# Two rows normalised inside the output projection, an earlier place for the first sigmoid, and four subtractions moved from GpSimd to VectorE

## The chip, the core and the metric

The kernel runs on one core of a Trainium2 chip. The core has a matmul engine (TensorE, PE in the profile, with its weight loads as PEld), a vector engine (VectorE, DVE), an engine for activation functions (ScalarE, ACT), a general engine (GpSimd, POOL) and a queue that only starts transfers (SyncE, SP). Each engine works through its own queue in order, and engines wait for each other by semaphores. A tile lies in SBUF, or, where PE writes it, in one of eight PSUM banks. The metric is the device time of one execution in microseconds; less is better.

## The reference

Two layers work on 512 tokens of 1024 features. Layer 0 projects the normalised tokens, runs a recurrence over them and a short convolution, and brings 2048 features back to 1024 with an output projection. Layer 1 is a convolution module. Around the border between the two the reference computes

```python
y = concatenate([ya * silu(za), yb * silu(zb)]) @ w_out       # layer 0, output projection
x = x + gate * rms_norm(y, g_post[0])                         # "post"
h = rms_norm(x, g_pre[1]) * (1 + scale) + shift               # "norm"
u, gl, z = split(h @ w_in, 3)                                 # layer 1, input projection
a = dwconv(u * sigmoid(gl), dw_w, 64) + dw_b                  # over segments of 64 tokens
```

Then follow a layer norm of `a`, `silu(a) * silu(z)`, and the second output projection. All is float32.

## The kernel before

**Precision.** A product of two float32 matrices is made of three matmuls (`mm3`, line 59): each operand is split into a high part, which ScalarE makes with a cast (line 126), and a low part, which is the operand less the high part (line 127). Line 127 subtracts on the engine that `env["lo"]` names: VectorE, or, for the weights of part 0 of the first 512 columns of layer 1, GpSimd (line 1115).

**Output projection.** `outproj` (line 130) multiplies two of the four rows of 128 tokens at a time: 16 steps (`ks`) of 12 matmuls of 512 columns, summed in four banks. The first call makes rows 0 and 1, in the banks `mm0`, `mm1` and the two of `at`; the second (line 1056) makes rows 2 and 3 in `uh0`, `uh1` and the two of `zo`, and starts with the three weight blocks that the first still holds. Each step loads 128 rows of the weight `wr` and of the activations `yr` through SP's queue, splits them into `wh`, `wl` and `y`, and has three sets of buffers for it.

**Rows.** Behind the second projection in the text stands a loop over the four rows (line 1060). `post` (line 1018) loads `x`, squares the row's two banks on ScalarE with a running sum, takes the square root (in `rstd`, line 1009) and the reciprocal, multiplies and adds on VectorE, and writes the row `x1d` for the end of layer 1. `norm` (line 1035) does the same with the new row: square, square root, reciprocal, product `xn`; then eight transposes of 128 by 128 on PE into the banks `at` (`h1t`, line 1046), eight activations that scale and shift (`hf`, line 1049), and the split into `h1h` and `h1l`.

**Layer 1.** For each of four groups of 512 columns (`n`), the weights are loaded and split (`wc...`, part 1 for `gl` and part 0 for `u`). Then, for each row `m`, 24 matmuls for part 1 and 24 for part 0 give two banks `pu`; the sigmoid of the first times the second is `a` (lines 1132 and 1133), which is split into `ah` (lines 1138 and 1139). The convolution is done with a short transform: `forward` multiplies `ah` with `dfc` into `px`, VectorE multiplies this with the transformed kernel `What` into `pr`, and `back` transforms it into `pc`. Both are put into a list, `late`, and run one after each of the next row's two parts. Banks for `pu` go round `mm0`, `mm1`, `uh0`, `uh1` (`dense`); `px` has the banks `zo` and `pc` the banks `at`.

**What sets the order.** The framework places instructions in the engines' queues ahead of time: whatever is earlier in the text comes first where it can run, and later work fills what the plan of times leaves empty. So the order in a queue isn't the order of the text, but the text gives the priority. Two means overrule it: `pinned()` (line 559) chains matmuls in the written order, used for `forward`, `back` and the products from `n + m = 2` on; and `tc.issue_after(ins)` places what is written in its block behind `ins` on the engine of `ins`. Tiles with one tag share a number of buffers (`BUFS`, line 992); a new tile waits until the old one's last reader is done.

Of the kernel before, what the change touches and what calls it, by code (L numbers as in the profile page):

```python
# [17 lines left out]
KT = 8  # L18
# [33 lines left out]
def kernel(ctx: ExitStack, tc: tile.TileContext, I: dict, out: bass.AP):  # L52
# [6 lines left out]
    def mm3(o, ah, al, bh, bl, start, stop, go=mm):  # L59
        go(o, ah, bh, start, False)  # L60
        go(o, ah, bl, False, False)
        go(o, al, bh, False, stop)
# [64 lines left out]
        env["lo"].tensor_tensor(out=lo, in0=raw, in1=hi, op=ALU.subtract)  # L127
        return hi, lo

    def outproj(m0, tags, ks, held, early=lambda k: (None, None, None)):  # L130
        acc = [[bank(f"o{m0 + m}{n}", tags[2 * m + n]) for n in range(2)] for m in range(2)]
        for k in ks:
            y, yr, ws = early(k)
            if y is None:
                y = op.tile([P, 512], F32R, tag="y", name=f"y{m0}_{k}", bufs=4)
            yh, yl = y[:, 0:256], y[:, 256:512]
            if (m0, k) == (0, 7):
                hilo(oT7[:, 0:256], None, yh, yl, None)
            else:
                if yr is None:  # L140
                    yr = op.tile([P, 256], F32, tag="yr", name=f"yr{m0}_{k}", bufs=4)
                hilo(ysp[k, :, m0 * P : m0 * P + 2 * P], yr, yh, yl)
            if k not in held:
                if ws is None:
                    ws = [op.tile([P, D], F32, tag="wr", name=f"wr{m0}_{k}", bufs=3)] + [
                        op.tile([P, D], F32R, tag="w", name=f"w{x}{m0}_{k}", bufs=6) for x in "hl"]
                held[k] = hilo(wo[k * P : (k + 1) * P, :], *ws)
            wh, wl = held[k]
            for m in range(2):
                ms = slice(m * P, (m + 1) * P)  # L150
                for n in range(2):
                    ns = slice(n * 512, n * 512 + 512)
                    mm3(acc[m][n], yh[:, ms], yl[:, ms], wh[:, ns], wl[:, ns], k == ks[0], k == ks[-1])
        return acc

    l0, rs = ExitStack(), ExitStack()
# [833 lines left out]
    with ExitStack() as l1:  # L990
# [3 lines left out]
        def lt(tag, name, dt=F32):  # L994
            return (lq if tag in ("xr", "pr") else lp).tile([P, 512 if tag in ("a", "pr") else D], dt, tag=tag, name=name,
                                                            bufs=BUFS[tag])
# [5 lines left out]
        def big(name, shape, dt=F32):  # L1002
            return lp.tile(shape, dt, tag=name, name=name)

        def dense(name):
            flip["mm"] = (flip["mm"] + 1) % 4
            return bank(name, ("mm0", "mm1", "uh0", "uh1")[flip["mm"]])

        def rstd(ssq, eps):
            S.activation(ssq[:, 2:3], ssq[:, 2:3], AF.Sqrt, bias=epsr[:, eps : eps + 1], scale=1.0 / D)  # L1010
            V.reciprocal(ssq[:, 3:4], ssq[:, 2:3])

        def gate_rows(layer):
            g = lq.tile([P, D], F32, tag="gg", name="gg1") if layer else lt("wz", "gg0")
# [3 lines left out]
        def post(m, pss, gg):  # L1018
            xr = lt("wz", f"x{m}")
            nc.gpsimd.dma_start(xr, I["x"][0, m * P : (m + 1) * P, :])  # L1020
            ssq = lp.tile([P, 4], F32, tag="ssq", name=f"ssqa{m}", bufs=4)
            t = lp.tile([P, D], F32, tag="pt", name=f"pta{m}", bufs=2)
            for n in range(2):
                S.activation(t[:, n * 512 : n * 512 + 512], pss[n], AF.Square, accum_out=ssq[:, n : n + 1])
            V.tensor_tensor(out=ssq[:, 2:3], in0=ssq[:, 0:1], in1=ssq[:, 1:2], op=ALU.add)
            rstd(ssq, 0)
            for n in range(2):
                sl = slice(n * 512, n * 512 + 512)
                V.scalar_tensor_tensor(out=t[:, sl], in0=pss[n], scalar=ssq[:, 3:4], in1=gg[:, sl],
                                       op0=ALU.mult, op1=ALU.mult)  # L1030
            V.tensor_tensor(out=xr, in0=xr, in1=t, op=ALU.add)
            nc.sync.dma_start(x1d[m], xr)
            return xr

        def norm(m, x1):
            ssq = lp.tile([P, 4], F32, tag="ssq", name=f"ssqb{m}", bufs=4)
            xn = lp.tile([P, D], F32, tag="pt", name=f"xn{m}", bufs=2)
            S.activation(xn, x1, AF.Square, accum_out=ssq[:, 2:3])
            rstd(ssq, 0)
            V.tensor_scalar(out=xn, in0=x1, scalar1=ssq[:, 3:4], scalar2=None, op0=ALU.mult)  # L1040
            for k4 in range(2):
                pt = bank(f"h1t{m}{k4}", "at")
                hf = lt("a", f"hf{m}{k4}").rearrange("p (k c) -> p k c", c=P)
                for k in range(4):
                    kt = 4 * k4 + k
                    T.transpose(pt[:, k * P : (k + 1) * P], xn[:, kt * P : (kt + 1) * P], ident)
                for k in range(4):
                    kt = 4 * k4 + k
                    S.activation(hf[:, k, :], pt[:, k * P : (k + 1) * P], AF.Identity, bias=modc1[:, kt : kt + 1],  # L1049
                                 scale=gsc1[:, kt : kt + 1])  # L1050
                ms = slice(m * P, (m + 1) * P)
                S.copy(h1h[:, 4 * k4 : 4 * k4 + 4, ms], hf)
                V.tensor_tensor(out=h1l[:, 4 * k4 : 4 * k4 + 4, ms], in0=hf, in1=h1h[:, 4 * k4 : 4 * k4 + 4, ms],
                                op=ALU.subtract)

        acc = outproj(2, ("uh0", "uh1", "zo", "zo"), ORDER[-3:] + ORDER[:-3], {k: held[k] for k in ORDER[-3:]})
        h1h = big("h1h", [P, KT, SEQ], F32R)
        h1l = big("h1l", [P, KT, SEQ], F32R)
        gg = gate_rows(0)
        for m in range(4):  # L1060
            x1 = post(m, (acc0 + acc)[m], gg)
            norm(m, x1)

        rs.close()
        lq = rs.enter_context(tc.tile_pool(name="lq", bufs=1, reuse_waits="tile", side="right"))
        w1_in = I["od_w_in"][0]
        dfw = lt("a", "dfw")[:, :NPROD]
        dfc = lt("pt", "dfc", F32R)
        dfh, dfl = dfc[:, :NPROD], dfc[:, NPROD : 2 * NPROD]
        dbe = big("dbe", [NPROD, 1])  # L1070
        dinv = big("dinv", [NPROD, 64])
        What = lq.tile([NPROD, EC], F32, tag="What", name="What")
        nc.gpsimd.dma_start(What, dwd)
        nc.gpsimd.dma_start(dfw, I["dfw"])
        S.copy(dfh, dfw)
        V.tensor_tensor(out=dfl, in0=dfw, in1=dfh, op=ALU.subtract)
        nc.gpsimd.dma_start(dbe, I["dbe"])
        nc.gpsimd.dma_start(dinv, I["dinv"])
        cres = [[lt("xr", f"cres{m}{q}") for q in range(2)] for m in range(4)]
        stats = big("stats", [P, 4, 4, 6])  # L1080
        tp = pinned()
        late = []

        def dft_stages(n, m, ahl):
            pr = [lt("pr", f"pr{n}{m}{s}") for s in range(2)]
# [20 lines left out]

            return forward, back

        for n in range(4):
            ws = {}  # L1110
            for part, tag in ((1, "wa"), (0, "wb")):
                for kt in range(0, KT, 2):
                    c0 = part * EC + n * 512
                    src = w1_in[kt * P : (kt + 2) * P, c0 : c0 + 512].rearrange("(a p) c -> p a c", p=P)
                    env["lo"] = G if n == 0 and part == 0 else V
                    w = split(src, f"wc{n}{part}{kt}", tag)
                    env["lo"] = V
                    for q in range(2):
                        ws[part, kt + q] = [t[:, q * 512 : q * 512 + 512] for t in w]
            for m in range(4):  # L1120
                ms = slice(m * P, (m + 1) * P)
                pp = []
                for part in (1, 0):
                    pu = dense(f"pu{n}{m}{part}")
                    for kt in range(KT):
                        wh, wl = ws[part, kt]
                        mm3(pu, h1h[:, kt, ms], h1l[:, kt, ms], wh, wl, kt == 0, kt == KT - 1, mm if n + m < 2 else tp)
                    pp.append(pu)
                    if late:
                        late.pop(0)()  # L1130
                a = lt("a", f"a{n}{m}")
                S.activation(a, pp[0], AF.Sigmoid)
                V.tensor_tensor(out=a, in0=pp[1], in1=a, op=ALU.mult)  # L1133
                ah = lt("wz", f"ah{n}{m}", F32R)
                ahl = [ah[:, 512 * s : 512 * s + 512] for s in range(2)]
                for s in range(2):
                    hr, lr = slice(64 * s, 64 * s + 64), slice(64 - 64 * s, 128 - 64 * s)
                    S.copy(ahl[s][hr], a[hr])  # L1138
                    V.tensor_tensor(out=ahl[s][lr], in0=a[hr], in1=ahl[s][hr], op=ALU.subtract)
                late.extend(dft_stages(n, m, ahl))  # L1140
        while late:
            late.pop(0)()
        for m in range(4):
# [159 lines left out]
```

## Time and profile before

| what | value |
|---|---|
| median of three runs | 1467.58 us (1464.46 to 1472.43) |
| the profiled execution | 1466.0 us, its span 1464.2 us |
| busy, share of the span | PE 96%, DVE 67%, ACT 51%, POOL 9% |
| granted clock of PE, mean | 0.978 |
| end of the second output projection | 1041.9 us into the span |

The span is what the profiler saw of the program's instructions; 1.8 us of the profiled execution's time lie outside it. A busy time is the time in which at least one instruction of the engine runs. "Line" numbers are those of the kernel before; a helper's line stands for all that call it, so the tile's name (output first, then the inputs) tells which work it is. The word behind an arrow is what an instruction waited for last.

### The profile page before, as it was taken

The numbers are of one execution on the slowest core, as the hardware profiler recorded it, in microseconds if no ns is written. First come the engines' busy times: TensorE is split into PE (matmuls) and PEld (weight loads), VectorE is DVE, ScalarE is ACT, GpSimd is POOL, SyncE is SP. The second block draws the span as 40 slices with busy tenths as digits, with TensorE's granted clock in tenths as the row PEclk, the third lists the DMA queues.
The fourth block names the chain that finished last, engine by engine and source line by source line (L and its number), as shares of the span: only waits on it lengthen the run. The fifth ranks groups of instructions, "written<-read, shape, count | busy, mean of one in ns | idle before, by whom it ended". The sixth has DMA issues, their size and how long they took to land. (4 is left out here: it accounts for less than half of the span.)

```text
span 1464.2 us, 29746 instructions
## 1 busy us (share of the span) xinstructions
PE 1408.5 (96%) x11921; PEld 1012.7 (69%) x11921; DVE 985.3 (67%) x2290; ACT 750.0 (51%) x1516; POOL 129.1 (9%) x250
## 2 busy tenths in 40 slices
PE   6899999999999999999999999999889999999998
PEld 1464677878776766666666666777767777788876
DVE  2675597567698989999999997557535535544333
ACT  4536364353655666656756655446643423463222
POOL 2023210000110101111011000011100000000000
PEclk9999999979897999999999999999989999999999
DMA  9755433312232312232222222468503303123322
GB/s 322 217 171 161 153 108 101 96 44 76 76 89 75 95 57 73 69 97 60 75 81 79 65 63 76 165 224 297 185 16 115 109 8 115 58 90 98 101 87 86
DMA packets 137626, 158.54 MB, mean 108 GB/s; under 512 B 15375, under 2 KB 104143, under 8 KB 137369
## 3 DMA queue, kind: packets, MB, share of 16 engines
q1 hardware_dynamic: 121104, 106.47, 23.5%
q0 software_dynamic: 15312, 48.99, 10.5%
q8 instruction: 93, 1.52, 0.4%
q10 hardware_dynamic: 1072, 1.19, 0.2%
q14 instruction: 45, 0.37, 0.1%
HBM read 138.33 MB, written 18.28 MB: 107 GB/s over the span
## 5 line engine op out<-in xcount | busy, mean ns | idle before, releaser
L57 PE MATMUL o<-wh,y 128*128 128x512 f32 x248 | 79.1, 396 | 0.0
L57 PE MATMUL pal<-ARl,BKl 64*128 64x128 f32 x512 | 58.1, 307 | 6.9 <-DVE xtmpc L654 2.9
L656 DVE TENSOR_TENSOR Yl<-Yl,xtmpl 128x126 f32<-128x126 f32 (+22 forms) x248 | 62.6, 252 | 2.7
L654 DVE TENSOR_TENSOR xtmpl<-Xl,Yl 128x126 f32<-128x126 f32 (+22 forms) x248 | 62.4, 252 | 2.7
L57 PEld LDWEIGHTS pal<-ARl,BKl 64*128 64x128 f32 x512 | 43.2, 195 | 26.3 <-issue 7.2
L1138 ACT CAST ah<-a 64x512 fp32r<-64x512 f32 x32 | 19.8, 619 | 72.9 <-DVE a L1133 72.4
L57 PE MATMUL zol<-UV,E 64*64 64x64 f32 (+1 forms) x1024 | 54.0, 221 | 0.2 <-ACT UV L762 0.2
L57 PE MATMUL o<-wl,y 128*128 128x512 f32 x124 | 49.6, 400 | 4.3 <-DVE wl L127 4.3
L127 DVE TENSOR_TENSOR wl<-wr,wh 128x1024 fp32r<-128x1024 f32 x28 | 38.1, 1361 | 23.1 <-ACT wh L126 22.7
L57 PEld LDWEIGHTS o<-wh,y 128*128 128x128 f32 x248 | 45.9, 188 | 9.6
L762 ACT COPY UV<-uh 64x128 f32<-64x128 f32 x128 | 33.4, 261 | 33.4 <-PE uh L57 25.8
L57 PE MATMUL zol<-Hl,ARl 64*64 64x64 f32 x896 | 50.2, 230 | 0.3
L57 PEld LDWEIGHTS zol<-Hl,ARl 64*64 64x64 f32 x896 | 35.0, 133 | 20.3 <-issue 16.7
L57 PEld LDWEIGHTS uh<-UV,BKt 128*64 128x64 f32 x704 | 26.7, 138 | 28.6 <-ACT UV L762 22.9
L599 DVE TENSOR_TENSOR E<-pal,maskE 128x512 f32<-128x512 f32 x64 | 43.1, 686 | 4.5 <-PE pal L57 4.2
L1133 DVE TENSOR_TENSOR a<-pu,a 128x512 f32<-128x512 f32 x16 | 11.0, 690 | 51.3 <-PE pu L57 49.0
L1094 DVE SCALAR_TENSOR_TENSOR pr<-px,dbe,What 119x512 f32<-119x512 f32 x32 | 22.6, 747 | 32.6 <-PE px L57 32.4
L57 PEld LDWEIGHTS zol<-UV,E 64*64 64x64 f32 (+1 forms) x1024 | 42.3, 136 | 2.6 <-ACT UV L762 2.0
L126 ACT CAST wh<-wr 128x1024 fp32r<-128x1024 f32 x28 | 29.4, 1051 | 23.5 <-DMA wr<-in_ev_w_out_dram 14.3
L873 POOL DMA_DIRECT2D mwr<-in_mod_w_dram x56 | 29.9, 539 | 113.9 <-PE uh L57 67.1
L769 DVE SCALAR_TENSOR_TENSOR Hl<-uh,PCl,HPl 128x64 f32<-128x64 f32 x112 | 26.5, 278 | 19.9 <-PE uh L57 9.7
L57 PE MATMUL uh<-UV,BKt 128*64 128x64 f32 x704 | 36.7, 234 | 2.2 <-ACT UV L762 2.2
(947 smaller groups left out, 4260.3 us busy)
## 6 DMA issues: line engine op xcount, KB each, us to landing
mwr<-in_mod_w_dram POOLq DMA_DIRECT2D x56, 256.0 KB, 3.8
wr<-in_ev_w_out_dram SPq DMA_DIRECT2D x28, 512.0 KB, 4.9
ectx<-in_mod_w_dram SPq DMA_DIRECT2D x12, 512.0 KB, 4.7
wrk<-in_ev_w_in_dram SPq DMA_DIRECT2D x16, 256.0 KB, 3.0
wrv<-in_ev_w_in_dram SPq DMA_DIRECT2D x16, 256.0 KB, 4.7
wrr<-in_ev_w_in_dram SPq DMA_DIRECT2D x16, 256.0 KB, 2.8
wrza<-in_ev_w_in_dram SPq DMA_DIRECT2D x16, 256.0 KB, 2.9
wrcg<-in_ev_w_in_dram SPq DMA_DIRECT2D x16, 256.0 KB, 2.9
```

The lines of the kernel that those rows point to most:

```text
L57: return T.matmul(o, lhsT, rhs, start=start, stop=stop)
L126: S.copy(hi, raw)
L127: env["lo"].tensor_tensor(out=lo, in0=raw, in1=hi, op=ALU.subtract)
L599: V.tensor_tensor(out=E[:, h, z * NLAT + c0 : z * NLAT + c0 + m, :], in0=pas[h], in1=maskE[:, z * (1 + h) : z * (1 + h) + 1, 0:x].to_broad ...
L654: V.tensor_tensor(out=tv, in0=X[:, :i, i : i + 1].to_broadcast([P, i, m]), in1=Y[:, i : i + 1, c0:].to_broadcast([P, i, m]), op=ALU.mult)
L656: V.tensor_tensor(out=Y[:, :i, c0:], in0=Y[:, :i, c0:], in1=tv, op=ALU.add)
L762: u_ = S.copy(UV[ZR[1 - h], i : 2 * nch - i : 2 * nch - 1 - 2 * i, ZR[h]], uh[ZR[1 - h], 0:2, :])
L769: h_ = V.scalar_tensor_tensor(out=Hn[:, z, :], in0=uh[:, 2 + z, :], scalar=PC[z][:, i : i + 1], in1=HP[:, z, :], op0=ALU.mult, op1=ALU.add)
L873: nc.gpsimd.dma_start(mws[q], I["mod_w"][layer, kt * P : (kt + 1) * P, c0 : c0 + 512])
L1094: V.scalar_tensor_tensor(out=pr[s][:NPROD], in0=px[s][:NPROD], scalar=dbe[:, 0:1], in1=What[:, n * 512 : n * 512 + 512], op0=ALU.add, op1= ...
L1133: V.tensor_tensor(out=a, in0=pp[1], in1=a, op=ALU.mult)
L1138: S.copy(ahl[s][hr], a[hr])
```

## The change

Five things, and the text they stand in:

1. `outproj` takes a table `between`, from a step to something that is run behind this step's matmuls. The second call has `rows(0)` (post and norm of row 0) behind step 13, its ninth, and `rows(1)` behind step 15, its eleventh. What these need (`h1h`, `h1l`, the gate row) is made ahead of the call; so are the small constants of the transform (`dfw`, `dfc`, `dbe`, `dinv`), which get tiles of their own.
2. The loop over `n` is taken apart into `weights`, `products` and `gated`. The weights and products of the first group and row are written ahead of row 2's and row 3's post and norm.
3. The first `gated` stands between row 3's post and its norm, and behind row 3's first square root (on ScalarE) and row 3's sum (on VectorE), which `post` leaves in `ordered`.
4. The pool that holds `What`, `cres` and `pr` is opened after row 3's norm, and `What` is loaded there.
5. `env["lo"]` stays on VectorE for all weights of layer 1.

```diff
-    def outproj(m0, tags, ks, held, early=lambda k: (None, None, None)):
+    def outproj(m0, tags, ks, held, early=lambda k: (None, None, None), between={}):
...
                     mm3(acc[m][n], yh[:, ms], yl[:, ms], wh[:, ns], wl[:, ns], k == ks[0], k == ks[-1])
+            if k in between:
+                between[k]()
...
         def rstd(ssq, eps):
-            S.activation(ssq[:, 2:3], ssq[:, 2:3], AF.Sqrt, bias=epsr[:, eps : eps + 1], scale=1.0 / D)
+            r_ = S.activation(ssq[:, 2:3], ssq[:, 2:3], AF.Sqrt, bias=epsr[:, eps : eps + 1], scale=1.0 / D)
             V.reciprocal(ssq[:, 3:4], ssq[:, 2:3])
+            return r_
...
-            V.tensor_tensor(out=xr, in0=xr, in1=t, op=ALU.add)
+            ordered[:] = [r_.ins, V.tensor_tensor(out=xr, in0=xr, in1=t, op=ALU.add).ins]
...
-        acc = outproj(2, ("uh0", "uh1", "zo", "zo"), ORDER[-3:] + ORDER[:-3], {k: held[k] for k in ORDER[-3:]})
+        w1_in = I["od_w_in"][0]
         h1h = big("h1h", [P, KT, SEQ], F32R)
         h1l = big("h1l", [P, KT, SEQ], F32R)
         gg = gate_rows(0)
-        for m in range(4):
-            x1 = post(m, (acc0 + acc)[m], gg)
-            norm(m, x1)
-
-        rs.close()
-        lq = rs.enter_context(tc.tile_pool(name="lq", bufs=1, reuse_waits="tile", side="right"))
...
-        dfc = lt("pt", "dfc", F32R)
+        dfc = big("dfc", [P, 2 * NPROD + 2], F32R)
...
+        def rows(m):
+            norm(m, post(m, acc0[m], gg))
+
+        order2 = ORDER[-3:] + ORDER[:-3]
+        acc = outproj(2, ("uh0", "uh1", "zo", "zo"), order2, {k: held[k] for k in ORDER[-3:]},
+                      between={order2[8]: lambda: rows(0), order2[10]: lambda: rows(1)})
...
-                    env["lo"] = G if n == 0 and part == 0 else V
                     w = split(src, f"wc{n}{part}{kt}", tag)
-                    env["lo"] = V
...
+        weights(0)
+        flip["mm"] = 3
+        pp = products(0, 0)
+        norm(2, post(2, acc[0], gg))
+        x1 = post(3, acc[1], gg)
+        with tc.issue_after(ordered[0]), tc.issue_after(ordered[1]):
+            first = gated(0, 0, pp)
+        norm(3, x1)
+        rs.close()
+        lq = rs.enter_context(tc.tile_pool(name="lq", bufs=1, reuse_waits="tile", side="right"))
+        What = lq.tile([NPROD, EC], F32, tag="What", name="What")
+        nc.gpsimd.dma_start(What, dwd)
+        cres = [[lt("xr", f"cres{m}{q}") for q in range(2)] for m in range(4)]
+        stats = big("stats", [P, 4, 4, 6])
+        late.extend(dft_stages(0, 0, first))
+        for n in range(4):
+            if n:
+                weights(n)
+            for m in range(n == 0, 4):
+                late.extend(dft_stages(n, m, gated(n, m, products(n, m))))
```

`products(n, m)` holds the two loops of matmuls and the calls of `late` between them, as they stood; `gated(n, m, pp)` holds the sigmoid, the product and the split into `ah`, as they stood.

More of the change, by code (lines that the diff above doesn't have):

```diff
@@ L1025, in post @@
             V.tensor_tensor(out=ssq[:, 2:3], in0=ssq[:, 0:1], in1=ssq[:, 1:2], op=ALU.add)
-            rstd(ssq, 0)
+            r_ = rstd(ssq, 0)
             for n in range(2):
@@ L1059 @@
         gg = gate_rows(0)
-        for m in range(4):
-            x1 = post(m, (acc0 + acc)[m], gg)
-            norm(m, x1)
-        rs.close()
-        lq = rs.enter_context(tc.tile_pool(name="lq", bufs=1, reuse_waits="tile", side="right"))
-        w1_in = I["od_w_in"][0]
+        ordered = []
         dfw = lt("a", "dfw")[:, :NPROD]
-        dfc = lt("pt", "dfc", F32R)
+        dfc = big("dfc", [P, 2 * NPROD + 2], F32R)
         dfh, dfl = dfc[:, :NPROD], dfc[:, NPROD : 2 * NPROD]
-        dbe = big("dbe", [NPROD, 1])
+        dbe = big("dbe", [P, 8])[:NPROD, 0:1]
         dinv = big("dinv", [NPROD, 64])
-        What = lq.tile([NPROD, EC], F32, tag="What", name="What")
-        nc.gpsimd.dma_start(What, dwd)
         nc.gpsimd.dma_start(dfw, I["dfw"])
@@ L1078 @@
         nc.gpsimd.dma_start(dinv, I["dinv"])
-        cres = [[lt("xr", f"cres{m}{q}") for q in range(2)] for m in range(4)]
-        stats = big("stats", [P, 4, 4, 6])
+        def rows(m):
[3 more added lines that the diff above has]
+                      between={order2[8]: lambda: rows(0), order2[10]: lambda: rows(1)})
         tp = pinned()
         late = []
+        ws = {}
         def dft_stages(n, m, ahl):
@@ L1107, in dft_stages, with weights @@
             return forward, back
-        for n in range(4):
-            ws = {}
+        def weights(n):
             for part, tag in ((1, "wa"), (0, "wb")):
@@ L1114 @@
                     src = w1_in[kt * P : (kt + 2) * P, c0 : c0 + 512].rearrange("(a p) c -> p a c", p=P)
-                    env["lo"] = G if n == 0 and part == 0 else V
                     w = split(src, f"wc{n}{part}{kt}", tag)
-                    env["lo"] = V
                     for q in range(2):
                         ws[part, kt + q] = [t[:, q * 512 : q * 512 + 512] for t in w]
[L1120 to L1140, printed above, removed]
@@ new lines, in products, with gated @@
+        def products(n, m):
+            ms = slice(m * P, (m + 1) * P)
+            pp = []
+            for part in (1, 0):
+                pu = dense(f"pu{n}{m}{part}")
+                for kt in range(KT):
+                    wh, wl = ws[part, kt]
+                    mm3(pu, h1h[:, kt, ms], h1l[:, kt, ms], wh, wl, kt == 0, kt == KT - 1, mm if n + m < 2 else tp)
+                pp.append(pu)
+                if late:
+                    late.pop(0)()
+            return pp
+        def gated(n, m, pp):
+            a = lt("a", f"a{n}{m}")
+            S.activation(a, pp[0], AF.Sigmoid)
+            V.tensor_tensor(out=a, in0=pp[1], in1=a, op=ALU.mult)
+            ah = lt("wz", f"ah{n}{m}", F32R)
+            ahl = [ah[:, 512 * s : 512 * s + 512] for s in range(2)]
+            for s in range(2):
+                hr, lr = slice(64 * s, 64 * s + 64), slice(64 - 64 * s, 128 - 64 * s)
+                S.copy(ahl[s][hr], a[hr])
+                V.tensor_tensor(out=ahl[s][lr], in0=a[hr], in1=ahl[s][hr], op=ALU.subtract)
+            return ahl
```

## The prediction

> **What bounds the kernel now.** I read the page first, then the windows around the edited code, then the waits of the matmul engine there, then the chain of waits and the timelines of each engine. The page says that TensorE is the bound:
>
> ```profile
> span 1464.2 us, 29746 instructions
> PE 1408.5 (96%) x11921; PEld 1012.7 (69%) x11921; DVE 985.3 (67%) x2290; ACT 750.0 (51%) x1516; POOL 129.1 (9%) x250
> ```
>
> So an edit of the schedule can only win back time in which PE stands still, or runs slowly. The windows (us, then busy time of PE, PEld, DVE, ACT, POOL, the granted clock, the DMA share, GB/s) find both in the edited stretch: the second output projection ends at about 1042, and layer 1's first products follow.
>
> ```profile
> 1000.00:1020.00 20.00, 18.07 (x78) 14.02 (x77) 18.96 (x24) 15.36 (x28) 6.31 (x3) 1.00 0.88 303
> 1020.00:1040.00 20.00, 17.60 (x76) 13.91 (x77) 14.21 (x15) 9.49 (x14) 4.98 (x2) 1.00 0.76 262
> 1040.00:1060.00 20.00, 18.64 (x91) 14.73 (x90) 8.48 (x17) 13.07 (x37) 1.10 (x2) 1.00 0.51 142
> 1060.00:1080.00 20.00, 14.75 (x60) 9.79 (x58) 10.36 (x16) 12.96 (x29) 0.55 (x1) 0.82 0.08 30
> 1080.00:1100.00 20.00, 20.00 (x82) 14.96 (x82) 7.10 (x9) 5.73 (x8) 0.00 (x0) 0.92 0.00 0
> ```
>
> The shortfalls of the first four rows are 1.93 + 2.40 + 1.36 + 5.25 = 10.9 us, and the granted clock is 0.82 and then 0.92 after the largest. The waits of PE between 980 and 1090 (total us, times, longest) name them:
>
> ```profile
> PE px L57 <- DVE ah L1139: 4.3, 1, 4.3
> PE o L57 <- DVE wl L127: 4.3, 4, 1.7
> PE h1t L1046 <- ACT hf L1049: 1.2, 1, 1.2
> PE pc L57 <- DVE pr L1094: 0.8, 1, 0.8
> PE pu L57 <- ACT h1h L1052: 0.2, 1, 0.2
> ```
>
> These five are all there is to win as idle time. What comes on top is the slow clock behind the first, which the chain of waits shows (start, us, what):
>
> ```profile
> 1074.61 2.25 PE px L57 x4
> ...
> 1077.65 2.62 PE pc L57 x8
> 1080.28 7.12 PE pu L57 x24
> 1087.39 0.89 PE px L57 x3
> 1088.28 5.80 PE pu L57 x24
> 1094.08 1.01 PE pc L57 x8
> ```
>
> The same three pieces cost 0.89, 1.01 and 5.80 us one row of tokens later. So the slow clock costs (2.25 - 0.89) + (2.62 - 1.01) + (7.12 - 5.80) = 4.3 us.
>
> **Part 1: GpSimd subtracts no weights.** Four subtractions for the columns of part 0 move from GpSimd to VectorE. GpSimd's four, and the VectorE instructions that ran beside them, with one undisturbed for comparison (start, us):
>
> ```profile
> 1009.18 2.61 POOL L127 TENSOR_TENSOR wc000l<-wc000r,wc000h 128x1024 fp32r<-128x1024 f32 x1 [0.32 <-ACT wc000h L126]
> 1015.59 3.15 POOL L127 TENSOR_TENSOR wc002l<-wc002r,wc002h 128x1024 fp32r<-128x1024 f32 x1 [3.80 <-ACT wc002h L126]
> 1031.99 2.40 POOL L127 TENSOR_TENSOR wc004l<-wc004r,wc004h 128x1024 fp32r<-128x1024 f32 x1 [13.24 <-ACT wc004h L126]
> 1035.14 2.58 POOL L127 TENSOR_TENSOR wc006l<-wc006r,wc006h 128x1024 fp32r<-128x1024 f32 x1 [0.75 <-ACT wc006h L126]
> 1010.31 2.56 DVE L127 TENSOR_TENSOR wl<-wr,wh 128x1024 fp32r<-128x1024 f32 x1
> 1017.47 2.36 DVE L127 TENSOR_TENSOR wl<-wr,wh 128x1024 fp32r<-128x1024 f32 x1 [1.00 <-ACT wh L126]
> 1020.94 1.22 DVE L127 TENSOR_TENSOR wl<-wr,wh 128x1024 fp32r<-128x1024 f32 x1
> 1032.85 2.62 DVE L127 TENSOR_TENSOR wl<-wr,wh 128x1024 fp32r<-128x1024 f32 x1 [2.85 <-ACT wh L126]
> 1035.39 2.61 DVE L127 TENSOR_TENSOR y<-yr,y 128x256 fp32r<-128x256 f32 x1
> ```
>
> Each GpSimd subtraction doubles a VectorE one that falls beside it, by 1.34, 1.14, 1.40 us, and stretches a small one to 2.61. Each of PE's four waits for wl sits right behind one of these four. VectorE saves 1.34 + 1.14 + 1.40 and about 2.2 (a y of a quarter of 1.22, by size about 0.4, took 2.61): 6.1 us. It takes on 4 x 1.22 = 4.9. The sum of its work is therefore unchanged, but no weight comes late by a doubled instruction. The doublings are worth 1.1 us or more each, the four waits 4.3 together and 1.7 at the longest, so 0.6 of that one could remain and little of the others. Bounds: all 4.3 us go, or none, since the weights also come by DMA (share 0.88 and 0.76 in the two windows) and the moved rows bring new work to VectorE and ScalarE here. I take 3.0, since all four waits stand behind a doubled instruction.
>
> **Part 2: rows 0 and 1 inside the projection.** Their sums and squares hardly move: they already run inside the projection. What moves in PE's queue is 16 transposes, from behind the last matmul of the projection to behind its ninth and eleventh step, and on ScalarE and VectorE what evacuates them. Now (PE's timeline):
>
> ```profile
> 1041.85 1.03 PE L1046 MATMUL h1t<-ident,xn 128*128 128x128 f32 x8
> 1044.04 0.66 PE L1046 MATMUL h1t<-ident,xn 128*128 128x128 f32 x4 [1.16 <-ACT hf L1049]
> 1044.89 0.50 PE L57 MATMUL pu<-wc010h,h1h 128*128 128x512 f32 x1 [0.20 <-ACT h1h L1052]
> ```
>
> The 16 transposes cost PE the same wherever they stand. The waits of 1.16 and 0.20 are saved: 1.4 us. The cost on the other engines, from the groups between 1041 and 1076 (busy us, mean ns):
>
> ```profile
> L1049 ACT ACTIVATE hf<-h1t,modc,gsc 128x128 f32<-128x128 f32 x32 | 12.3, 480 | 9.4 <-PE h1t L1046 9.4
> L1052 ACT CAST h1h<-hf 128x512 fp32r<-128x512 f32 x8 | 5.2, 651 | 0.0
> ```
>
> Half of each, 6.2 + 2.6 = 8.8 us of ScalarE, and four VectorE subtractions, join the window 1020 to 1040, where ScalarE is busy 9.49 of 20 and VectorE 14.21. Both have room; the weights' casts queue behind them on the in-order ScalarE, with three steps of buffers as cover. That cover is why I charge nothing here; if it is gone, the loss is the 4.3 us of part 1 again. On the queues: GpSimd's gets the dfw load (one issue) ahead of the four loads of x, SP's the two x1d writes among the weight loads, as now, since these writes wait for sums that hardly move. The load of What moves behind row 3 in the written order, but waits for the same thing as now, the projection's buffers; nothing stands behind it.
>
> **Part 3: the first sigmoid.** Today it runs on ScalarE behind row 3's whole normalisation, and this one waits for transposes that stand in PE's queue behind products of rows 0 and 1:
>
> ```profile
> 1066.39 1.85 ACT L1049 ACTIVATE hf<-h1t,modc,gsc 128x128 f32<-128x128 f32 x5 [2.28 <-PE h1t L1046]
> 1069.83 1.28 ACT L1132 ACT_TABLE_LOAD   x1
> 1071.12 0.60 ACT L1132 ACTIVATE a<-pu 128x512 f32<-128x512 f32 x1
> 1073.87 2.84 DVE L1139 TENSOR_TENSOR ah<-a,ah 64x512 fp32r<-64x512 f32 x4
> ```
>
> After the change it stands behind row 3's first square root and before row 3's second. The first 48 products end about 11.6 us after the projection (twice 5.80). Then comes the product with a (some 0.7 us), two casts and two subtractions: half of the 2.84, so about 2.7 us with what is beside it, and up to 4.4 (half of 8.8) if one row's hf and h1h go first on ScalarE. PE has 24 products (5.8) and 16 transposes (twice 1.03 at most, I take 1.7, since they overlap what follows) before it needs ah: 7.5 against 2.7 to 7.1. So the wait of 4.3 goes, the wait of 0.8 for pr goes (the other half of the row's products then stands between), and with them the 4.3 of slow clock: 9.5 us. Bounds: nothing is won if ah still comes last, 9.5 if it comes in time; I take 8.5, one microsecond off for the thin cover.
>
> The price is table loads: the second square root of row 3 follows the first sigmoid, and the next sigmoid follows that, so two more loads of 1.28 us each on ScalarE. They hide in ScalarE's idle time (7 of 20 in each of the two windows from 1040), and row 3's columns are wanted only after 144 products. If they were on the path, they would take 2.6 off. The Trainium skill, page "ScalarE: Activation LUTs", section "What ACT_TABLE_LOAD costs", gives 1283 ns for the load and 1380 ns more for a drain at each switch. The trace has the load, but from its start at 1069.83 to the sigmoid at 1071.12 there is no room for the drain; by the page two switches on the path would take 5.3 off, and the sum below would be 7.6 instead of 10.3.
>
> **Sum.** 3.0 + 1.4 + 8.5 = 12.9 us off. From 1087 on PE is busy without a gap (20.00 of 20 in the last window), so the gain passes to the end. The profiled execution took 1466.0 us (1464.2 and 1.8 around the span): 1453.1. The median of the three runs, 1467.58, lies 1.6 higher, so I predict 1454.7 for a median. If all the waits and the slow clock go, 4.3 + 1.4 + 9.5 = 15.2 is won: 1452.4, or 1450.8 from the profiled execution.
>
> **Rivals.** (a) ah stays late. For it: ScalarE is in order, and the normalisation of row 2 stands ahead of the casts. Against: the sum above leaves 4.8 us of cover, and still 0.4 in the worst order. Only 3.0 + 1.4 is won: 1463.2. The Trainium skill, page "TensorE: Matmul & The Clock Gate", Part 1, has the clock fall after an idle window of about 3.4 us; the trace agrees so far, as the wait of 1.7 us left the clock at 1.00 and that of 4.3 did not; by it, a remainder of a wait below that would cost only itself.
>
> (b) The projection stays bound by its weights: ScalarE's extra 8.8 us delay the casts, the 4.3 of waits stay and perhaps double. For it: a DMA share of 0.88, VectorE busy 18.96 of 20 in the first window. Against: VectorE loses as much as it gains. Won is 8.5 + 1.4 - 0 to 4.3: 5.6 to 9.9, 1457.7 to 1462.0.
>
> (c) Slower: PE is in order too, and the transposes now stand between matmuls of the projection. If they come up in the queue before their row is normalised, PE stands still with ready matmuls behind. A row's chain, from the first square to the normalised row, undisturbed:
>
> ```profile
> 1049.55 0.68 ACT L1024 ACTIVATE pta<-o 128x512 f32<-128x512 f32 x1
> 1057.17 0.75 DVE L1040 TENSOR_SCALAR xn<-x,ssqb 128x1024 f32<-128x1024 f32 x1
> ```
>
> That is 8.4 us. If PE waits the whole chain at both rows, and each time pays 4.3 of slow clock, it loses 25.4; against the 12.9 won that is 12.5 more: 1480.1. It decides from 12.9 us of such waits on, and is measurable from 20.2. For it: row 0's transposes need the two banks that hold row 1's sums, so they need row 1's sums read as well. Against: both rows' sums are complete when the projection starts, and the first row is placed nine steps of 12 matmuls in. By this piece of the chain
>
> ```profile
> 969.08 29.03 PE o L57 x127
> ```
>
> a matmul takes 0.229, so that is 24.7 us, against a chain of 8.4 for one row.
>
> (d) The order on the engines stays, or one row waits as in (c): 12.9 - 12.7, so 1467.4.
>
> **How the numbers follow.** The forecast gets 0.59, with its own range 1450 to 1460; (a) 0.12, (b) 0.11, (c) 0.13, (d) 0.05. Half a per cent, 7.3 us, is what a measurement of this kernel tells from no change, so faster is below 1460.2: the forecast and a good half of the lighter (b), 0.64. Same: (a), the heavier (b) and (d), 0.23. Slower: (c), 0.13. The range 1450 to 1467 leaves out (c), half of (d) and 0.03 below: 0.19.
>
> **What would show it.** No GpSimd subtraction between 1000 and 1040, and wl at 1.22 throughout (part 1). Eight transposes twice between o matmuls, without a wait in front, and pu right behind the last o (part 2). A sigmoid before the last square root on ScalarE, two more table loads, px without a wait, and a clock of 1.00 where 0.82 stood (part 3). I am wrong if PE waits for xn or ah for more than 5 us together, or if the o matmuls still wait 4 us for wl.

## The result, and the profile after

The changed kernel takes 1451.79 us (median of 7 runs, 1448.18 to 1460.24) against 1467.06 us before (7 runs, 1463.35 to 1472.43). The ratio is 0.9907, with a 95% interval of 0.9882 to 0.9933. The profiled execution has a span of 1449.6 us against 1464.2. The page of the changed kernel:

```profile
span 1449.6 us, 29729 instructions
PE 1407.2 (97%) x11921; PEld 1012.7 (70%) x11921; DVE 983.7 (68%) x2294; ACT 749.5 (52%) x1516; POOL 118.2 (8%) x246
```

VectorE has four instructions more and GpSimd four fewer; PE has the same work and less time in which to do it. The windows (us, busy time of PE, PEld, DVE, ACT, POOL, granted clock, DMA share, GB/s):

```profile
1000.00:1020.00 20.00, 19.78 (x92) 15.96 (x91) 17.91 (x26) 14.99 (x27) 0.53 (x1) 1.00 0.90 309
1020.00:1040.00 20.00, 18.53 (x84) 14.59 (x83) 16.50 (x22) 19.02 (x40) 0.00 (x0) 1.00 0.74 246
1040.00:1060.00 20.00, 20.00 (x95) 16.02 (x94) 10.70 (x18) 12.36 (x29) 1.06 (x2) 1.00 0.62 178
1060.00:1080.00 20.00, 20.00 (x93) 14.26 (x91) 7.66 (x12) 5.77 (x13) 0.00 (x0) 1.00 0.00 1
```

PE is short of 1.7 us over the four, where it was 10.9, and the clock of 0.82 is gone. ScalarE is now full from 1020 to 1040 (19.02), with the transposes' evacuation in it. What PE still waits for in this stretch (total us, times, longest):

```profile
PE o L57 <- DVE wl L127: 1.2, 3, 0.7
PE h1t L1049 <- ACT hf L1052: 0.5, 1, 0.5
```

The waits for ah, for pr and for h1h are not there any more. The chain of waits, from the end of layer 0 on (start, us, what; the last line is row 1's `pc`):

```profile
967.39 1.15 PE po L57 x32
...
1040.33 11.19 PE pu L57 x48
...
1059.78 0.23 PE px L57
...
1065.78 1.01 PE pc L57 x8
1066.79 5.79 PE pu L57 x24
...
1079.25 1.01 PE pc L57 x8
```

I use two marks in it for every kernel below: the start of the last `po`, a group of small matmuls at the end of layer 0, and the start of row 1's `pc`. The way between them holds all that the change touches and leaves out layer 0, whose length differs from run to run (the start of the last `po` lies between 961.3 and 974.5 us in the profiles of this study). Each way comes from one trace. Before, the first mark stands here:

```profile
967.93 1.15 PE po L57 x32
```

So the way was 1094.08 - 967.93 = 126.2 us and is 1079.25 - 967.39 = 111.9: 14.3 of the 14.6 us lie in it. From the prediction's rows and these, the wait for wl gives 4.3 - 1.2 = 3.1, the waits around the transposes 1.4 - 0.5 = 0.9, those for ah and pr 5.1, and the slow clock 4.3: 13.4 together, 0.9 stays unassigned.

The order on ScalarE is not the one that the prediction had:

```profile
1050.55 0.29 ACT L1012 ACTIVATE ssqb<-ssqb,epsr 128x1 f32<-128x1 f32 x1
...
1055.44 1.28 ACT L1134 ACT_TABLE_LOAD   x1
1056.73 0.60 ACT L1134 ACTIVATE a<-pu 128x512 f32<-128x512 f32 x1
```

The first sigmoid stands behind row 3's second square root, not before it, and there is one table load here, not three. And the transposes of rows 0 and 1 stand inside the projection (PE's timeline, the first at 1017):

```profile
1017.03 1.03 PE L1049 MATMUL h1t<-ident,xn 128*128 128x128 f32 x8
...
1024.40 0.60 PE L1049 MATMUL h1t<-ident,xn 128*128 128x128 f32 x4
...
1025.46 0.66 PE L1049 MATMUL h1t<-ident,xn 128*128 128x128 f32 x4 [0.46 <-ACT hf L1052]
```

### The profile page after: what moved, and what is told of

The parts are those of the page before. It is cut to its first block, busy times and chain, and to the rows that moved or that the text cites. A ratio compares the mean times of both kernels' runs of the same rounds, so it can differ in the third digit from the quotient of the medians.

```text
span 1449.6 us, 29729 instructions
## 1 busy us (share of the span) xinstructions
PE 1407.2 (97%) x11921; PEld 1012.7 (70%) x11921; DVE 983.7 (68%) x2294; ACT 749.5 (52%) x1516; POOL 118.2 (8%) x246
## 5 line engine op out<-in xcount | busy, mean ns | idle before, releaser
L127 DVE TENSOR_TENSOR wl<-wr,wh 128x1024 fp32r<-128x1024 f32 x28 | 34.2, 1223 | 19.6 <-ACT wh L126 19.1
```

## The experiments

The change has three parts that can be made alone: the subtractions (1), rows 0 and 1 inside the projection (2), the first row's products and sigmoid ahead of row 3's norm (3). Six kernels are the changed one with one or two parts undone. Undoing them takes these edits:

```diff
 # without part 1, in weights(n)
+                    env["lo"] = G if n == 0 and part == 0 else V
                     w = split(src, f"wc{n}{part}{kt}", tag)
+                    env["lo"] = V
 # without part 2
-        acc = outproj(2, ("uh0", "uh1", "zo", "zo"), order2, {k: held[k] for k in ORDER[-3:]},
-                      between={order2[8]: lambda: rows(0), order2[10]: lambda: rows(1)})
+        acc = outproj(2, ("uh0", "uh1", "zo", "zo"), order2, {k: held[k] for k in ORDER[-3:]})
+        rows(0)
+        rows(1)
 # without part 3
+        norm(2, post(2, acc[0], gg))
+        norm(3, post(3, acc[1], gg))
         weights(0)
         flip["mm"] = 3
         pp = products(0, 0)
-        norm(2, post(2, acc[0], gg))
-        x1 = post(3, acc[1], gg)
-        with tc.issue_after(ordered[0]), tc.issue_after(ordered[1]):
-            first = gated(0, 0, pp)
-        norm(3, x1)
+        first = gated(0, 0, pp)
```

### Parts 1 and 2, without part 3

> Parts 1 and 2 without part 3: rows 2 and 3 are normalised first, and weights, products and sigmoid of the first row are written behind them. Theory A (the prediction's): part 3 is what takes the wait for ah away, so without it px waits 4 us or more again, the clock falls behind it, and the span is 8 to 9.5 us above the changed kernel's 1449.6, at 1458 to 1459. Theory B: part 2 is enough for that. With rows 0 and 1 off ScalarE and PE, row 3's transposes stand behind 52 products instead of some 80, and PE's queue has px behind 84 products, so ah comes in time with a wait of at most 1 us: 1449.5 to 1451.5.

Measured: 1450.77 us, ratio 0.9881 (0.9849 to 0.9914), span 1449.4, way 1078.99 - 966.71 = 112.3. PE doesn't wait for ah at all. Theory A, the prediction's, is wrong here: without part 3 nothing that can be measured is lost.

### Parts 1 and 3, without part 2

> Parts 1 and 3 without part 2: all four rows are normalised behind the projection. Theory A (terms add up): only the wait for the first transposes comes back, about 1 us and some of the restart, 1450.5 to 1452. Theory C: part 3 needs part 2, since ScalarE evacuates rows 0 and 1 ahead of the sigmoid, and px waits 2 to 4 us: 1454 to 1458.

Measured: 1456.28 us, ratio 0.9943 (0.9918 to 0.9968), span 1452.9, way 117.7 (117.2 without two products of the next step that stand before the mark here). That is 5.4 us longer than the changed kernel's. The size is that of theory C (4 to 8 us above the changed kernel's span), but not its reason: PE doesn't wait for ah, but for other things, which the run of part 3 alone shows below.

### Part 1 alone

> Part 1 alone: only the four subtractions go from GpSimd to VectorE. Theory A: the waits of the projection for wl fall from 4.3 to about 1 us, the wait for ah (4.3) and the slow clock stay: span 1460.5 to 1461.5. Rival: the weights are late by their transfers, the waits for wl stay at 4: 1464.

Measured: 1462.72 us, ratio 0.9984 (0.9955 to 1.0013), span 1462.2, way 123.5: 2.6 us less than before. PE waits 1.6 us for wl instead of 4.3, and 4.4 for ah. Theory A holds in the trace; the time alone couldn't tell it from no change.

### Parts 2 and 3, without part 1

> Parts 2 and 3, GpSimd subtracts as before. Theory A: VectorE instructions beside GpSimd's double again, o waits 4 us or so for wl, and the moved rows are hit too: span 1452 to 1455. Rival (transfers): o waits as in the changed kernel, 1.2 us, and the span is 1449.6.

Measured: 1452.00 us, ratio 0.9903 (0.9874 to 0.9933), way 113.1, 1.2 more than the changed kernel's, which lies between the two expectations. (The span of 1457.2 has its excess in layer 0: the first mark stands at 973.48.) PE waits for wl

```profile
PE o L57 <- DVE wl L127: 2.1, 5, 0.7
```

half of what it waited before, though GpSimd subtracts as before. VectorE's timeline shows what GpSimd doubles now:

```profile
1020.93 2.62 DVE L127 TENSOR_TENSOR y<-yr,y 128x256 fp32r<-128x256 f32 x1
...
1044.67 3.41 DVE L127 TENSOR_TENSOR wc110l<-wc110r,wc110h 128x1024 fp32r<-128x1024 f32 x1
```

These are two of the four, and PE waits right behind neither. The other two are `wl` as before (2.57 and 2.73 us), with a wait of 0.7 us behind each. So what GpSimd's subtractions cost depends on which VectorE instruction happens to stand beside them. The Trainium skill, page "SBUF — State Buffer", section "SBUF: two separate sides", has the two engines take a shared port in turn, each for a whole instruction, where the VectorE instruction has two SBUF inputs. The trace agrees: before, the doubled instructions are subtractions of two SBUF tiles, and a product with a PSUM bank that ran beside GpSimd's first subtraction took 0.75 us, as the others do.

### Part 2 alone

> Part 2 alone: rows 0 and 1 inside the projection, GpSimd subtracts, the first row's products and sigmoid stay behind row 3's norm. Theory A (part 3 removes the wait for ah): only 1 us is won, 1463. Theory B (part 2 is enough): the wait of 4.3 and the slow clock go too, 1453 to 1456.

Measured: 1452.19 us, ratio 0.9913 (0.9884 to 0.9942), way 1075.87 - 961.83 = 114.0: 12.1 us less than before by this part alone. Theory B holds. All that PE waits for:

```profile
PE o L57 <- DVE wl L127: 1.9, 4, 0.7
PE h1t L1049 <- DVE xn L1043: 0.9, 1, 0.9
```

How part 2 takes the wait for ah away can be read from three rows of the timeline (ScalarE, PE, ScalarE) and one of the chain of waits:

```profile
1033.67 0.60 ACT L1027 ACTIVATE pta<-o 128x512 f32<-128x512 f32 x1 [1.67 <-PE o L57]
...
1049.94 1.06 PE L1049 MATMUL h1t<-ident,xn 128*128 128x128 f32 x8
...
1055.34 0.60 ACT L1136 ACTIVATE a<-pu 128x512 f32<-128x512 f32 x1
```

```profile
1058.48 0.24 PE px L57
```

The projection's last matmul starts at 1035.30 here and at 1041.61 before. Row 3's transposes come 14.6 us after it, before it was 24.1; the sigmoid, still behind them on ScalarE, 20.0 after it instead of 29.5; px, without a wait, 23.2 after it instead of 33.0. What moved first is row 2's first square on ScalarE: it starts 1.6 us ahead of the last matmul's start here (1033.67), and 7.9 us after it before (1049.55), since ScalarE there evacuates rows 0 and 1 first, from 1042.48 on. That is 9.6 us, and all the rest follows by nearly as much. PE's queue isn't what held row 3's transposes: they start 0.15 us after the end of its product `xn` in both kernels (1065.57 to 1065.72 before, 1049.79 to 1049.94 here).

Not all of the 12.1 us come this way. The wait for ah, the wait for pr and the slow clock make 9.4; the wait for wl fell by 2.4, since GpSimd's subtractions now stand beside other instructions, as in the kernel above.

### Part 3 alone

> Part 3 alone: the first row's products and sigmoid ahead of row 3's norm, rows 0 and 1 behind the projection, GpSimd subtracts. Theory A: the wait of 4.3 and the slow clock go, 1454 to 1456. Theory C (part 3 needs part 2): px still waits 2 to 4 us, 1458 to 1462.

Measured: 1462.26 us, ratio 0.9968 (0.9941 to 0.9996), way 121.2 (120.7 with the same correction as above): 5.4 us less than before. The wait for ah is gone, as theory A said, but not its gain; the time is near theory C's range, but without its wait. PE waits for these (and twice 0.2 us):

```profile
PE o L57 <- DVE wl L127: 4.0, 3, 2.2
PE h1t L1049 <- ACT hf L1052: 1.2, 1, 1.2
PE pc L57 <- ACT hf L1052: 1.2, 1, 1.2
PE h1t L1049 <- DVE xn L1043: 0.9, 1, 0.9
```

The third and the fourth are new: `pc` needs a bank `at`, and row 3's transposes, now late, hold both. The first costs more than its 4.0 us. Its longest piece, 2.15, brings the clock down (PE's timeline, the last line at full clock for comparison):

```profile
1037.40 0.66 PE L57 MATMUL o<-wl,y 128*128 128x512 f32 x1 [2.15 <-DVE wl L127]
1037.86 1.05 PE L57 MATMUL o<-wh,y 128*128 128x512 f32 x2
...
1042.08 0.63 PE L57 MATMUL o<-wh,y 128*128 128x512 f32 x2
```

The nine matmuls from 1037.40 on take 3.75 us; the nine behind the wait of 1.7 us before the change took 2.18. So this wait, behind a `wl` that GpSimd's subtraction doubled to 2.62, costs 1.6 us of slow clock on top. Here are the two more table loads that the prediction charged to part 3 (ScalarE's timeline):

```profile
1064.88 1.28 ACT L1137 ACT_TABLE_LOAD   x1
...
1069.49 1.28 ACT L1012 ACT_TABLE_LOAD   x1
1070.79 0.29 ACT L1012 ACTIVATE ssqb<-ssqb,epsr 128x1 f32<-128x1 f32 x1
...
1078.59 1.28 ACT L1137 ACT_TABLE_LOAD   x1
```

They come with part 3 only where part 2 is missing. The second stands right ahead of row 3's square root, and so in the way of the transposes that PE waits for.

The six, the kernel before and the changed one make a table of the way, in us:

| | without part 2 | with part 2 |
|---|---|---|
| neither 1 nor 3 | 126.2 | 114.0 |
| 1 | 123.5 | 112.3 |
| 3 | 120.7 | 113.1 |
| 1 and 3 | 117.2 | 111.9 |

Part 2 is worth 12.1 alone and 5.4 as the last. Part 3 is worth 5.4 alone, and 1.0 or 0.4 once part 2 is in. Part 1 is worth 2.6 and 3.5 without part 2, 1.8 and 1.2 with it; the 3.5 hold the 1.6 us of slow clock that, of these eight, only part 3 alone shows in the projection. The kernel before also lacks items 2 and 4 of the change, which all six have. They are worth nothing that shows: part 1 alone differs from it by 2.6 us, and its waits for wl by 2.7.

### Rows 0 and 1 earlier, and later

```diff
-                      between={order2[8]: lambda: rows(0), order2[10]: lambda: rows(1)})
+                      between={order2[3]: lambda: rows(0), order2[4]: lambda: rows(1)})    # early
+                      between={order2[13]: lambda: rows(0), order2[15]: lambda: rows(1)})  # last
```

> The changed kernel with rows 0 and 1 behind the fourth and fifth step of the projection instead of the ninth and eleventh. From the last po to row 1's pc the changed kernel takes 111.9 us. If PE's queue gets the transposes only where the rows are ready, waits stay under 1 us and this is 111.5 to 113. If they come up ahead of their rows (rival c), PE waits for xn or h1t, 2 to 8 us a row, with matmuls of the projection ready behind: 115 to 125.

Measured: 1453.15 us, ratio 0.9923 (0.9895 to 0.9951), way 1080.43 - 965.77 = 114.7, 2.8 more than the changed kernel's. This is rival (c) of the prediction in small: the transposes come up in PE's queue before their banks are free, and the clock falls behind the wait (PE's timeline, and the windows around it):

```profile
1005.85 0.66 PE L1049 MATMUL h1t<-ident,xn 128*128 128x128 f32 x4 [2.38 <-DVE pta L1032]
```

```profile
1003.00:1005.00 2.00, 0.47 (x3) 0.05 (x1) 2.00 (x6) 2.00 (x5) 0.00 (x0) 1.00 0.94 342
1005.00:1007.00 2.00, 1.15 (x10) 1.07 (x10) 2.00 (x5) 2.00 (x4) 0.53 (x1) 1.00 0.95 309
1007.00:1009.00 2.00, 2.00 (x7) 1.53 (x6) 2.00 (x3) 2.00 (x7) 0.00 (x0) 0.54 0.96 348
1009.00:1011.00 2.00, 2.00 (x7) 1.62 (x6) 2.00 (x4) 2.00 (x5) 0.00 (x0) 0.61 0.84 232
```

What PE waits for, at one of the two rows, is VectorE's product of row 1's sums (`pta`), which lie in the banks `at`, as the prediction said of (c).

> The same with rows 0 and 1 behind the fourteenth and the last step. If it is enough that rows 0 and 1 stand ahead of rows 2 and 3 in priority, nothing changes: 112 to 113. If ScalarE's time behind the projection is what counts (theory B: rows 0 and 1 have to be off it), half of the gain over the kernel of part 3 goes, px waits for ah or row 0 for its h1h, 2 to 4 us: 114 to 117.

Measured: 1448.01 us, ratio 0.9901 (0.9869 to 0.9932), way 1073.13 - 961.27 = 111.9, the same as the changed kernel's. Row 0's transposes run 6.9 us ahead of the start of the projection's last matmul (1032.49), and row 1's right behind it:

```profile
1025.64 1.04 PE L1049 MATMUL h1t<-ident,xn 128*128 128x128 f32 x8
...
1032.72 1.03 PE L1049 MATMUL h1t<-ident,xn 128*128 128x128 f32 x8
```

ScalarE squares row 2 (from 1032.90) before it evacuates row 1 (from 1034.59). So it isn't needed that both rows are off ScalarE when the projection ends; one row's evacuation still fits behind it. To stand ahead of rows 2 and 3 in the text isn't enough, though: rows 0 and 1 do so in parts 1 and 3 without part 2 as well, where 5.4 us are lost. In the two kernels with places from the ninth step to the last, the way is the same.

### How much the slow clock costs, and from which wait on

Four kernels make ah late by copies of `a` onto itself on ScalarE, which add work and change nothing in the result:

```diff
...
             V.tensor_tensor(out=a, in0=pp[1], in1=a, op=ALU.mult)
+            for _ in range(again):     # first gated(0, 0) only: 6, 8, 12 or 18
+                S.copy(a, a)
...
```

> The changed kernel with twelve extra copies of a onto itself on ScalarE between the first product and its split, so that ah comes 6 to 7 us later and px 1.5 to 3 us too late. If the clock falls only behind a wait of 3.4 us or more, the granted clock stays 1.00, px and pc cost 0.9 and 1.0 us, and the loss is the wait for ah, the 0.8 for pr, and little more: 1452 to 1454. If any wait costs clock, px, pc and the 24 products behind them are slow: 4 us more.

> The same with eighteen copies, so that px waits 4.5 to 6 us. By either rule the clock falls: px and pc take 2.2 and 2.6 us, the 24 products 7.1, about 4.3 us on top of the waits: 1458 to 1461.

Measured with twelve: 1457.15 us (one run), a wait of 5.3 for ah, way 121.0. With eighteen: 1471.36 us (one run; its layer 0 was long as well, with the first mark at 974.51), a wait of 9.1, way 124.5. Both waits are longer than intended, and in both the clock falls. px, pc and the 24 products behind them take 2.26, 2.62 and 6.60 us with twelve, and 2.25, 2.63 and 6.74 with eighteen, against 0.89, 1.01 and 5.80. So the slow clock costs 3.8 and 3.9 us, as little behind 9.1 us of wait as behind 5.3 (and 4.3 before the change, behind 4.3).

> The changed kernel with eight copies of a. From 5.3 us of wait with twelve and 9.1 with eighteen, 0.63 each, the wait for ah is 2.8. If the clock falls only behind longer waits, px and pc cost 0.9 and 1.0 us and the way from the last po to row 1's pc is 114 to 115.5. If any wait costs it, px and pc take over 2 us and the way is 118 to 119.

> Six copies: a wait of 1.5 us. Clock 1.00 by the first rule, 113 to 114; by the second 116 to 117.

Measured with eight: 1452.70 us (one run), waits of 1.9 and 0.2 for ah and 1.1 for pr, way 117.4. With six: 1456.47 us (one run), 0.4 for ah and 1.6 for pr, way 116.1. The clock falls in both, and the ways are near the second rule's, so the first rule, that only a wait of 3.4 us or more costs clock, doesn't hold here. With six copies (windows of 2 us):

```profile
1068.00:1070.00 2.00, 1.66 (x9) 0.67 (x9) 1.94 (x4) 0.31 (x1) 0.00 (x0) 1.00 0.00 0
1070.00:1072.00 2.00, 2.00 (x6) 1.61 (x6) 1.06 (x2) 0.59 (x1) 0.00 (x0) 0.54 0.04 8
1072.00:1074.00 2.00, 2.00 (x7) 1.52 (x7) 0.00 (x0) 0.00 (x0) 0.00 (x0) 0.61 0.00 0
```

But the second rule, that any wait costs it, doesn't hold either. In the kernel of part 3 alone the waits of 0.9 and 1.2 lie close together, and the clock stays:

```profile
1072.00:1074.00 2.00, 1.14 (x8) 0.71 (x7) 1.40 (x4) 0.00 (x0) 0.00 (x0) 1.00 0.00 0
1074.00:1076.00 2.00, 0.84 (x10) 0.53 (x9) 0.00 (x0) 1.85 (x6) 0.00 (x0) 1.00 0.00 0
1076.00:1078.00 2.00, 2.00 (x14) 1.32 (x11) 0.69 (x1) 2.00 (x7) 0.00 (x0) 1.00 0.04 8
```

About 2 us of idle time in 4 cost clock in one kernel and not in the other. What parts them is where fixed windows of time begin and end. A slow clock is half the full one, as in these two rows of the kernel before:

```profile
1074.00:1076.00 2.00, 1.39 (x2) 0.54 (x2) 1.93 (x3) 1.29 (x3) 0.00 (x0) 0.50 0.00 0
1076.00:1078.00 2.00, 1.16 (x4) 0.56 (x4) 1.84 (x3) 0.00 (x0) 0.00 (x0) 0.50 0.00 0
```

So the length of a slow stretch follows from the clock of the windows that hold it. With six copies it is (2 x 0.46 + 2 x 0.39) / 0.5 = 3.4 us, and the same with rows 0 and 1 early. Before the change it is 10.2 (from 1072.92 to 1083.16), with twelve copies 10.2, with eighteen 13.7: one, three and four times 3.41. In every trace of this study, all slow stretches, those of layer 0 too, begin a whole number of times 3.41 us apart (before, from 448.29 to 1072.92, it is 183 times). The clock here changes at the ends of windows of 3.41 us that run on through the whole program.

What counts then is PE's idle time in one such window. In the window ahead of the fall it is 1.4 us with eight copies, 1.6 with six, 2.1 with rows 0 and 1 early, 2.15 in the projection with part 3 alone, and 2.4 to 3.2 behind the waits of 4.3 and more. The waits of 0.9 and 1.2, which left the clock alone, lie in two windows, with 1.4 and 0.6 us. There is no sharp line between: windows with 1.6 us (before, at the wait of 1.7 for wl) and 1.8 (eight copies, one window earlier) left the clock alone too. Why 1.4 was enough once and 1.8 was not stays open.

One thing needed no run: without the two `issue_after` lines around the first `gated`, all five engines get the same instructions in the same order. The planner puts the sigmoid there by itself.

## Why the prediction was right, and where it was wrong

**The time.** Forecast were 1454.7 us and 12.9 us off; measured are 1451.8, and 14.3 us off in the stretch. The waits and the slow clock were read from the right rows, and they went as listed (0.5 us at the transposes and 1.2 for wl stayed). What was wrong is which part takes which of them away.

**Part 1, right in size.** Forecast 3.0; the wait for wl fell by 3.1, and the part alone wins 2.6. That each wait stood behind a doubled instruction was the right sign. What the step lacked is that the same four subtractions cost only 1.2 to 1.8 once part 2 has moved other work beside them, so in the changed kernel part 1 adds less than half of its 3.0.

**Part 2, wrong by its reason.** The step said that 16 transposes move and 1.4 us of waits are saved, and it looked for the cost of the moved work only where it arrives (ScalarE from 1020 to 1040). It didn't ask what the work leaves behind. Part 2 alone wins 12.1 us, 9.4 of them since it makes room on ScalarE for rows 2 and 3, and with them for the sigmoid behind row 3. The prediction had quoted half of the link itself: the sigmoid waits behind row 3's transposes. It took these to stand in PE's queue behind products; they start 0.15 us after row 3's own `xn`, and what made that late was ScalarE, busy with rows 0 and 1.

**Part 3, wrong in what it does.** It got 8.5 us; it wins 5.4 alone and 0.4 as the last. The order forecast for ScalarE (sigmoid before row 3's second square root) is not the one in the changed kernel. With the order that came instead, the two extra table loads fell away too; they appear with part 3 where part 2 is missing, and there the first sigmoid does come earlier. Each of the two parts takes the wait for ah away by itself, and the sum came out because the wait was counted once. That is luck as far as part 3 goes: its 8.5 us would have come without it (way 112.3).

**The cover of ah.** Taken as thin, with 1 us off for it. In the changed kernel px comes without any wait, so all of the 9.5 was won, though not by the order that the cover was worked out for.

**Rivals.** (a) and (b) didn't come. For (b), the projection's waits are 1.2 us, with ScalarE busy 19.02 of 20 in the window where its 8.8 us arrived. (c) exists: four or five steps into the projection it costs 2.8 us, not at nine and eleven. The sentence beside (a), that a remainder below 3.4 us would cost only itself, is refuted for this kernel by the runs with six and eight copies, and by the wait of 2.15 us with part 3 alone.

## What to carry to other kernels

When work moves from one stage to another, work out the stage that it leaves as carefully as the one it enters: what stood behind it on each in-order engine moves up, and that can be the larger gain. When two edits may feed the same wait, price each of them with the other absent and present; a right sum doesn't show that the parts are right. And compare kernels that differ by a few microseconds by the way between two marks in the trace that enclose the edit: here the way told differences of 1 us, while whole runs of one kernel differ by 10 and more.

## What the runs showed of the hardware that wasn't expected

The slow clock of TensorE comes behind waits shorter than thought, and at fixed times. A single wait of 2.4 us between matmuls of the projection brought it down 1.3 us after work had begun again (0.54 and 0.61 in the two windows from 1007 on), one of 2.15 us with part 3 alone 0.2 us after, and 2.0 us in three pieces did the same (0.54 and 0.61 from 1070 on); a wait of 1.7 us before the change, and 2.0 us in two pieces in the kernel of part 3 alone, did not. The Trainium skill, page "TensorE: Matmul & The Clock Gate", Part 1, gives an idle window of about 3.4 us for the fall, and has the windows run freely. The second agrees with the traces, where slow stretches begin whole multiples of 3.41 us apart. The first differs: no window ahead of a fall in this stretch was idle throughout, and 1.4 to 2.15 us of idle time in it were enough four times. So a slow matmul needn't touch the gap that made it slow.

The price follows the same windows. One slow window costs at most half of 3.41, 1.7 us (1.6 measured in the projection with part 3 alone). Behind the long waits the clock stays slow for three or four windows, and yet the price hardly grows, 3.8 us for a wait of 5.3 and 3.9 for 9.1, since much of the wait itself lies in the slow stretch. In each case of this stretch the clock came back at the end of the first window in which PE had less than 0.02 us of idle time; before the change, the wait of 0.8 for pr stood in the slow window just before that one.
